# Log-sum-exp kernel: the heads of the last fourteen tiles shared out anew among four engines, three TensorE heads in the last row, no waits between the PSUM banks of a pair

## Chip, cores and metric

One core of a Trainium2 chip. The metric is the device time of one execution in microseconds (us), the median of several; the kernel before takes 327.5 us. The profiled span of the same execution is about 1.8 us shorter than its time.

## The reference, cut to what matters

```python
B, S, D, H = 8, 2048, 2048, 8          # x: (B, S, D) float32, bias: (H, D // H)
x_heads = x.reshape(B, S, H, D // H).transpose(0, 2, 1, 3) + bias[None, :, None, :]
x_tiled = np.repeat(x_heads, 2, axis=2)
mx = x_tiled.max(axis=-1, keepdims=True)
lse = mx.squeeze(-1) + np.log(np.exp(x_tiled - mx).sum(axis=-1))   # (8, 8, 4096)
```

Each of the 8 x 2048 rows holds 8 heads of 256 numbers. For every head: add a bias vector, exponentiate, sum, take the logarithm, write it twice. 134 MB are read, 1 MB is written.

## The kernel before, as far as it matters here

64 tiles of 2 MB (128 partitions x 2 rows x 2048), nine buffers. A head can be done in three ways, and the kernel shares the eight heads of a row among the engines by stage:

- **TensorE head**: TensorE puts the bias into a PSUM bank (a matmul of ones with three bf16 parts of the bias) and adds x (a matmul with the identity, float32). ScalarE exponentiates and sums in one instruction.
- **Weighted head**: ScalarE exponentiates x alone; VectorE multiplies by exp(bias), which lies in PSUM, and sums.
- **Added head**: GpSimd adds the bias in SBUF, ScalarE exponentiates, VectorE reduces.

```python
BULK = dict(pe=3, acc=1, g0=4, late=True, fold=0)        # whole tiles, 3 TensorE heads, 4 added
MIXED = dict(pe=1, acc=1, g0=4, late=False, fold=0)      # 1 TensorE head, 3 weighted, 4 added
PROMPT = dict(pe=2, acc=2, g0=8, late=False, fold=0)     # 2 TensorE heads, 6 weighted
PROMPT_F1 = dict(pe=2, acc=2, g0=8, late=False, fold=1)  # the last head folded by GpSimd
PROMPT_F2 = dict(pe=2, acc=2, g0=8, late=False, fold=2)  # the last two
STAGES = [
    (0, (BULK,)), (50, (MIXED,)),
    (56, (MIXED, MIXED)),                                # from here half tiles, one row each
    (61, (PROMPT, PROMPT)), (62, (PROMPT, PROMPT_F1)), (63, (PROMPT_F2, PROMPT)),
]
LAST_COLS = [                                            # column pieces of the two last rows
    [(0, 512), (1280, 2048), (512, 1280)],
    [(0, 512), (512, 1024), (1024, 1536), (1536, 2048)],
]
...
pairs = [pp.tile([P, 2 * MM], F32, name=f"pair{i}") for i in range(2)]
ps = [p[:, c : c + MM] for p in pairs for c in (0, MM)]  # four banks in two tiles of two banks
...
def sum_biased(m, t, k, p, mm, sums):                    # ScalarE's part of a TensorE head
    for h in range(m["pe"]):
        c = h * Dh
        act = nc.scalar.activation(out=xts[t % NBUF][:, k, c : c + Dh], in_=p[:, c : c + Dh],
            func=ACT.Exp, accum_out=sums[:, k, h : h + 1])
        last_uses[t].append(on_x(t, act, [mm]))
...
def fold(t, k, h0, h1, sums, after):                     # GpSimd: times exp(bias), then 256 -> 32
    v = xts[t % NBUF][:, k, h0 * Dh : h1 * Dh]
    done = nc.gpsimd.tensor_tensor(out=v, in0=v, in1=w_sb[...], op=ALU.mult)
    ...
    while n > FOLD:
        n //= 2
        done = nc.gpsimd.tensor_tensor(out=v[:, :, 0:n], in0=v[:, :, 0:n],
                                       in1=v[:, :, n : 2 * n], op=ALU.add)
    # VectorE sums the remaining 32, one unit later
```

For one half tile the order is: TensorE adds x and puts the next half's bias; ScalarE exponentiates the weighted heads of this half, then does the TensorE heads of the half before; VectorE weighs.

The softmax here doesn't subtract the row's maximum and nothing guards it: scores larger than these inputs give would overflow.

## Time and profile before

| | kernel before |
|---|---|
| time, median (range) | 327.52 us (327.40 to 327.56) |
| busy: TensorE, VectorE, ScalarE, GpSimd | 77%, 88%, 81%, 89% |
| DMA rate over the span | 416 GB/s |
| last piece of x lands | 319.45 us |
| sums complete | 322.00 us |
| span | 325.5 us |

How to read it: four engines look nearly full, yet none of them sets the pace over the 300 us in the middle; the loads do, and nine buffers keep them some 30 us ahead. So I read the end: the last landings, the chain behind them, and the TensorE clock there. The lines stand in the prediction. In them L307 is ScalarE's exponential of x, L282 its part of the TensorE heads, L342 a weighted head on VectorE, L326 and L372 VectorE's reductions, L358 GpSimd's fold, and L408 the closing transpose.

The median of 327.52 us is that of the three executions known when the prediction was written; a fourth, run with the changed kernel, makes it 327.46 (the table after the prediction).

### The profile page before, as it was taken

What the parts mean: (1) busy time and instruction counts of PE and PEld (TensorE: products, weight loads), DVE (VectorE), ACT (ScalarE), POOL (GpSimd) and SP (SyncE); (2) the same over time, 40 slices, a digit from 0 to 9 for tenths busy, and PEclk for the clock granted to TensorE, in tenths of its full rate; (3) what the DMA queues carried; (4) which work ended last, traced back from release to release, by engine and by line L of the source; (5) the groups of instructions that cost most, each with busy time, mean ns of one, the idle gap of its engine ahead of it and who ended that gap; (6) DMA issues with size and microseconds to landing.
All of it is one profiled execution on the core that took longest, in us unless ns stands there. A gap on an engine that the chain in (4) does not pass through costs nothing.

```text
span 325.5 us, 2113 instructions
## 1 busy us (share of the span) xinstructions
PE 250.0 (77%) x541; PEld 86.9 (27%) x541; DVE 285.9 (88%) x320; ACT 264.3 (81%) x421; POOL 289.9 (89%) x88
## 2 busy tenths in 40 slices
PE   4478999499987888777879797889788455576792
PEld 1123333233322323223323232223223101122220
DVE  1006999999999999999898899989998999999995
ACT  1119999499978969888787978697879897799995
POOL 6999999799999999999999999999999999999713
PEclk9999999899979979998997989797979855555558
DMA  8999999999999999999999999999999999999994
GB/s 293 427 431 429 431 429 424 431 427 429 429 429 429 427 426 429 429 423 430 432 425 429 431 422 427 431 427 429 429 431 425 429 432 424 413 422 421 422 400 143
DMA packets 11806, 135.42 MB, mean 416 GB/s; under 512 B 1361, under 2 KB 1489, under 8 KB 2833
## 3 DMA queue, kind: packets, MB, share of 16 engines
q1 hardware_dynamic: 11696, 135.27, 98.6%
q8 instruction: 4, 0.07, 0.1%
q14 instruction: 8, 0.07, 0.0%
q10 hardware_dynamic: 2, 0.01, 0.0%
q0 software_dynamic: 96, 0.00, 0.0%
HBM read 134.23 MB, written 1.05 MB: 416 GB/s over the span
## 4 chain that ended last, share of the span: by engine, by line
DMA 48%; DVE 33%; ACT 8%; POOL 6%; PE 3%; issue 1%; SPq 0%; DVEq 0%
DMA xt<-in_x_dram 45%; DVE R L326 27%; ACT xt L307 6%; DVE xt L319 4%; POOL xt L301 4%; DMA b<-bparts 2%; PE pair L249 1%; PE one_ps L249 1%; DVE xt L342 1%; ACT xt L282 1%; DMA brow<-in_bias_dram 1%; ACT xt L267 1%; POOL brest L173 1%; POOL brest L171 1%; PE pair L203 0%
## 5 line engine op out<-in xcount | busy, mean ns | idle before, releaser
L301 POOL TENSOR_TENSOR xt<-xt,b_rep 128x2048 f32<-128x2048 f32 (+1 forms) x66 | 277.3, 4210 | 18.9 <-DMA xt<-in_x_dram 18.9
L326 DVE TENSOR_REDUCE R<-xt 128x14 f32<-128x3584 f32 (+1 forms) x56 | 208.1, 3716 | 2.6 <-ACT xt L307 0.9
L307 ACT ACTIVATE xt<-xt 128x2560 f32<-128x2560 f32 (+3 forms) x91 | 164.2, 1828 | 14.8 <-POOL xt L301 14.3
L249 PE MATMUL pair<-xt,ident 128*128 128x512 f32 x200 | 105.5, 654 | 0.0
L249 PE MATMUL one_ps<-xt,ident 128*128 128x512 f32 x100 | 61.0, 695 | 19.9 <-DMA xt<-in_x_dram 19.8
L267 ACT ACTIVATE xt<-pair 128x1024 f32<-128x1024 f32 x50 | 52.3, 1045 | 17.2 <-PE pair L249 15.8
L249 PEld LDWEIGHTS pair<-xt,ident 128*128 128x128 f32 x200 | 42.4, 212 | 56.0 <-issue 56.0
L319 DVE TENSOR_TENSOR xt<-xt,w_ps 128x512 f32<-128x512 f32 x50 | 34.0, 680 | 25.6 <-ACT xt L307 25.4
L233 PE MATMUL pair<-xt,ident 128*128 128x512 f32 (+1 forms) x44 | 34.0, 872 | 21.2 <-DMA xt<-in_x_dram 18.2
L260 ACT ACTIVATE xt<-one_ps 128x256 f32<-128x256 f32 x100 | 37.7, 394 | 8.1 <-PE one_ps L249 8.1
L203 PE MATMUL one_ps<-b,ones 3*128 3x512 bf16 x50 | 19.0, 381 | 17.9 <-ACT xt L260 11.8
L203 PEld LDWEIGHTS <-ones 3*128 3x128 bf16 x150 | 12.5, 92 | 65.7 <-issue 59.7
L203 PE MATMUL pair<-b,ones 3*128 3x512 bf16 x100 | 29.9, 378 | 0.0
L249 PEld LDWEIGHTS one_ps<-xt,ident 128*128 128x128 f32 x100 | 15.6, 197 | 41.3 <-DMA xt<-in_x_dram 34.1
L260 ACT ACTIVATION_READ_ACCUMULATOR xt<-one_ps 128x1 f32 x100 | 22.1, 221 | 0.0
L342 DVE CUSTOM_DVE_ANT_0 xt<-xt,one_ps 128x256 f32<-128x256 f32 x50 | 19.1, 414 | 0.3 <-ACT xt L307 0.3
L233 PEld LDWEIGHTS pair<-xt,ident 128*128 128x128 f32 x44 | 10.4, 294 | 29.6 <-DMA xt<-in_x_dram 19.7
L342 DVE CUSTOM_DVE_ANT_0 xt<-xt,w_ps 128x256 f32<-128x256 f32 x45 | 17.5, 417 | 0.0
L282 ACT ACTIVATE xt<-pair 128x256 f32<-128x256 f32 x34 | 12.5, 374 | 0.1
L326 DVE TENSOR_REDUCE R_last<-xt 128x4 f32<-128x1024 f32 x10 | 12.1, 1214 | 0.0
L218 PE MATMUL pair<-b,ones 3*128 3x512 bf16 (+1 forms) x22 | 10.2, 465 | 1.1 <-ACT xt L267 1.1
L358 POOL TENSOR_TENSOR xt<-xt,w_sb 128x256 f32<-128x256 f32 (+1 forms) x2 | 2.1, 1026 | 8.7 <-ACT xt L307 8.5
(38 smaller groups left out, 55.9 us busy)
## 6 DMA issues: line engine op xcount, KB each, us to landing
xt<-in_x_dram SPq DMA_DIRECT2D x56, 2048.0 KB, 29.9
xt<-in_x_dram SPq DMA_DIRECT2D x14, 1024.0 KB, 21.0
xt<-in_x_dram SPq DMA_DIRECT2D x5, 256.0 KB, 11.4
out_dram<-res SPq DMA_DIRECT2D x1, 896.0 KB, 7.3
xt<-in_x_dram SPq DMA_DIRECT2D x2, 384.0 KB, 16.5
out_dram<-res_last SPq DMA_DIRECT2D x1, 128.0 KB, 1.7
b<-bparts POOLq DMA_DIRECT2D x3, 1.5 KB, 6.5
brow<-in_bias_dram ACTq DMA_DIRECT2D x1, 8.0 KB
```

Source lines behind the costliest of these rows:

```text
L203: nc.tensor.matmul(p, lhsT=ones3, rhs=each_row(b3, h * Dh, Dh, K), start=True, stop=False,)
L218: nc.tensor.matmul(p, lhsT=ones3, rhs=each_row(b3, 0, n, kb - ka), start=True, stop=False,)
L233: mm = nc.tensor.matmul(p, lhsT=ident, rhs=xts[t % NBUF][:, ka:kb, 0:n], start=False, stop=True,)
L249: mm = nc.tensor.matmul(p, lhsT=ident, rhs=xts[t % NBUF][:, :, h * Dh : (h + 1) * Dh], start=False, stop=True,)
L260: act = nc.scalar.activation(out=xts[t % NBUF][:, k, 0:Dh], in_=got[0][:, k * Dh : (k + 1) * Dh], func=ACT.Exp, accum_out=sums[:, k, 0:1],)
L267: act = nc.scalar.activation(out=xts[t % NBUF][:, :, Dh : m["pe"] * Dh].rearrange("p k (h j) -> p h k j", j=Dh), in_=got[-1].rearrange("p ...
L282: act = nc.scalar.activation(out=xts[t % NBUF][:, k, c : c + Dh], in_=p[:, c : c + Dh], func=ACT.Exp, accum_out=sums[:, k, h : h + 1],)
L301: add = nc.gpsimd.tensor_tensor(out=v, in0=v, in1=each_row(b_rep, c - G0, D - c, k1 - k0), op=ALU.add)
L307: return on_x(t, nc.scalar.activation(out=v, in_=v, func=ACT.Exp), [after])
L319: mul = nc.vector.tensor_tensor(out=f, in0=f, in1=each_row(w_ps, m["pe"] * Dh - W0, n, k1 - k0), op=ALU.mult,)
L326: red = nc.vector.tensor_reduce(out=sums[:, k0:k1, h0:H], in_=v.rearrange("p k (h j) -> p k h j", j=Dh), op=ALU.add, axis=mybir.AxisListTy ...
L342: ttr = nc.vector.tensor_tensor_reduce(out=v, in0=v, in1=w, scale=1.0, scalar=0.0, op0=ALU.mult, op1=ALU.add, accum_out=dst,)
```

## The change

The intent: keep the cheap bulk stage longer, relieve GpSimd of its slow bias adds in the half tiles, and use all engines evenly in the last tile.

```diff
-PROMPT = dict(pe=2, acc=2, g0=8, late=False, fold=0)
+SINGLE_F1 = dict(pe=1, acc=1, g0=8, late=False, fold=1)
+TRIPLE = dict(pe=3, acc=3, g0=8, late=False, fold=0)
 STAGES = [
     (0, (BULK,)),
-    (50, (MIXED,)),
-    (56, (MIXED, MIXED)),
-    (61, (PROMPT, PROMPT)),
-    (62, (PROMPT, PROMPT_F1)),
-    (63, (PROMPT_F2, PROMPT)),
+    (54, (MIXED,)),
+    (57, (PROMPT_F1, PROMPT_F1)),
+    (62, (SINGLE_F1, SINGLE_F1)),
+    (63, (PROMPT_F2, TRIPLE)),
 ]
 LAST_COLS = [
     [(0, 512), (1280, 2048), (512, 1280)],
-    [(0, 512), (512, 1024), (1024, 1536), (1536, 2048)],
+    [(0, 512), (768, 1280), (1280, 1792), (512, 768), (1792, 2048)],
 ]
...
+    bank_users = [[], []]
+    def on_bank(i, ins):
+        for j, u in bank_users[i // 2]:
+            if j != i and u.ins.engine != ins.ins.engine:
+                tc.declare_no_dep(ins.ins, u.ins, reason="another bank")
+        bank_users[i // 2].append((i, ins))
+        return ins
... (put_bias, add_x and sum_biased call it; a row of three heads takes two banks; the
...  TensorE heads of a row may now come in two pieces)
```

## The prediction

> **What bounds the kernel now.** I read the page first, for engine shares and the slices, then the chain that ended last, then the timelines of single engines over the last 20 us, then the groups by form.
>
> The page (PEclk is the granted TensorE clock in tenths, GB/s the DMA rate, 40 slices of 8.1 us):
>
> ```profile
> span 325.5 us, 2113 instructions
> PEclk9999999899979979998997989797979855555558
> GB/s 293 427 431 429 431 429 424 431 427 429 429 429 429 427 426 429 429 423 430 432 425 429 431 422 427 431 427 429 429 431 425 429 432 424 413 422 421 422 400 143
> HBM read 134.23 MB, written 1.05 MB: 416 GB/s over the span
> ```
>
> From the second slice to the last but one the rate is flat: 134 MB of input pass at some 428 GB/s, and no edit of who computes what changes the bytes. The trace's record of landings says the same: whole tiles (2 MB) land 4.89 us apart, half tiles 2.48 us apart, and the last piece of x lands at 319.45 us. The loads run six or more tiles ahead, so a late engine in the middle costs nothing. What remains to win or lose is what follows the last landings. The second thing to see is the clock: half from slice 32 on, in the stage that this change rebuilds.
>
> The chain that ended last (start, us, what), from 305 us on:
>
> ```profile
> 294.41 19.82 DMA xt<-in_x_dram
> ...
> 314.26 1.48 ACT xt L307
> 315.74 1.46 ACT xt L282 x8
> 317.20 1.47 ACT xt L307 x2
> ...
> 318.69 0.42 DVE xt L342
> ...
> 321.86 0.14 DVE R_last L372
> 322.00 0.14 issue
> 322.14 0.32 PE tpair L408
> ```
>
> DMA sets the time until tile 62's second half lands (314.24). Then ScalarE has a queue, its four TensorE heads lying ahead of the exponentials of the last tile, and VectorE starts the last nine heads only at 318.69. The sums are complete at 322.00; transpose, logarithm, store and end take another 3.5 us (325.5 - 322.0), which the change leaves alone. So I ask one thing: when are the sums complete afterwards?
>
> Timeline of TensorE (L218 writes the bias, L233 adds x; start, busy us):
>
> ```profile
> 299.36 1.22 PE L233 MATMUL pair<-xt,ident 128*128 128x256 f32 x2 [0.93 <-DMA xt<-in_x_dram]
> 300.51 0.39 PE L218 MATMUL pair<-b,ones 3*128 3x256 bf16 x1
> ...
> 309.36 2.08 PE L233 MATMUL pair<-xt,ident 128*128 128x512 f32 x2
> 311.37 0.60 PE L218 MATMUL pair<-b,ones 3*128 3x512 bf16 x1
> 311.90 2.08 PE L233 MATMUL pair<-xt,ident 128*128 128x512 f32 x2
> ...
> 317.89 1.12 PE L233 MATMUL pair<-xt,ident 128*128 128x512 f32 x2
> ```
>
> At half clock two heads hold TensorE for 2.01 us (309.36 to 311.37) and their bias for 0.53 (to 311.90), 2.54 us a half tile against 2.48 of DMA; one head takes 1.15 (299.36 to 300.51). At full clock, from 315.9 on, two heads take 1.12.
>
> Groups by form (busy us, mean ns):
>
> ```profile
> L342 DVE CUSTOM_DVE_ANT_0 xt<-xt,w_ps 128x256 f32<-128x256 f32 x45 | 17.5, 417 | 0.0
> L326 DVE TENSOR_REDUCE R<-xt 128x8 f32<-128x2048 f32 x6 | 13.7, 2283 | 0.9 <-ACT xt L307 0.9
> L307 ACT ACTIVATE xt<-xt 128x1536 f32<-128x1536 f32 x10 | 14.6, 1471 | 0.3 <-DMA xt<-in_x_dram 0.3
> L307 ACT ACTIVATE xt<-xt 128x768 f32<-128x768 f32 x12 | 9.9, 835 | 0.0
> L358 POOL TENSOR_TENSOR xt<-xt,w_sb 128x256 f32<-128x256 f32 x1 | 0.8, 779 | 8.5 <-ACT xt L307 8.5
> ```
>
> These give the unit costs. A weighted head on VectorE is 417 ns, and such heads start 0.343 us apart (318.69 to 321.78 for nine). An exponential of 1536 elements is 1.47 us, of 768 0.835, so 0.83 ns an element; in a row each starts 0.09 us before the last one ends. A TensorE head summed by ScalarE takes 0.36 us in a row, and the last one ends 0.5 us after its start. A one-head fold on GpSimd is 0.78 us and three adds, 2.12 us from start to next possible start.
>
> **What the Trainium skill says.** "TensorE: Matmul & The Clock Gate", Part 1: half clock is the idle state, judged in free-running windows of about 3.4 us. The trace agrees: every change of the granted clock lies on a 3.41 us grid. Summing in each window the matmuls that add x, I find that 0.99 and more of a half-clock window was followed by full clock, 0.84 was not; at full clock 0.56 and less was followed by half, 0.59 was not. "SBUF - State Buffer", Who interferes with whom: a VectorE instruction with two SBUF inputs contends with GpSimd's reads, one with a single SBUF input doesn't. The weights of heads 2 to 6 lie in PSUM, and the trace agrees: the heads keep 0.34 us beside GpSimd's adds (270 to 281 us) and without them. "PSUM - Partial Sum Buffer", bank collisions: guard by bank and quadrant; dropping waits between different banks is allowed. No wait of this kind is large in the trace: TensorE's L233 waited for ScalarE once, 3.0 us.
>
> **The change part by part.**
>
> Stages. Bulk runs to tile 53 instead of 49, the mixed whole tiles are 54 to 56, half tiles begin at 57. Bulk VectorE work is 0.60 + 3.89 = 4.5 us a tile against 4.89 of DMA, so this part stays hidden. One split fewer saves 2 x 2.48 - 4.89 = 0.07 us of DMA.
>
> GpSimd's bias add. Ten half-tile adds of 2.36 us go, and with them on ScalarE a second exponential (1024 elements) and on VectorE a reduce of 1.21 us per half. In their place each half of tiles 57 to 61 costs VectorE 5 x 0.343 + about 0.17 (last reduce of the fold) = 1.9 us (before 3 x 0.343 + 1.21 - about 0.08 = 2.15), ScalarE 1.39 + 2 x 0.36 = 2.1, GpSimd 2.12, all under 2.48. At half clock TensorE is at 2.54 and falls behind by 0.06 a half, 0.6 in ten, which tile 62 with one head makes up.
>
> Do they arrive in time? In the kernel before VectorE starts the first mixed tile 7.2 us after its landing (261.75 - 254.54). Afterwards that start is 274.55 + 7.2 = 281.75. Three mixed tiles at 4.24 end at 294.5, ten halves at 1.9 at 313.5, the six heads and reduce of tile 62's first half at 315.7. GpSimd: its last add ends at 284.4 + 4.54 = 288.9, the first fold starts at about 292.3 (after two exponentials), eleven folds of 2.12 end at 315.6. ScalarE: 62's second half, 1792 elements, lands at 314.2 and is through at 314.2 + 1.69 = 315.9. All three meet within 0.4 us there; no backlog, and no reserve either.
>
> The end, VectorE. From 315.9: six heads and a reduce to 318.2, then heads 5; 2, 3, 4; 3, 4; 5, 6; 7: nine times 0.343 = 3.09, to 321.3, and the last reduce 0.2: 321.5. That is 0.5 us better than 322.00: one head of tile 62 comes to VectorE, ScalarE's queue shrinks by two heads.
>
> The end, ScalarE. Exponential to 315.8, two heads of tile 62 to 316.5, 768 + 768 elements to 318.0, row 0's two heads to 318.7, then 512, 512 and 256 elements (0.52, 0.52, 0.31) to 320.06, three heads of the last row, the last starting at 320.8: 321.3, if TensorE has delivered.
>
> The end, TensorE. With one head in tile 62 TensorE's share of x falls to 1.15 / 2.48 = 0.46, so by the windows above the half clock will stand in the last tile, where the kernel before had full clock, earned by two heads in each of tiles 61 and 62. In order from the landing at 314.2: one head 1.15, bias 0.53, row 0's two heads 2.01, bias of the last row on two banks 0.9, its first two heads 2.01, its third 1.2: 322.0. ScalarE then needs 0.5 for the last head: 322.5. At full clock the same order waits for landings only and TensorE is done by 319.8.
>
> Sum: sums complete at max(321.5, 321.3, 322.5) = 322.5 instead of 322.0 at half clock, and 321.5 at full clock: 327.52 + 0.5 = 328.0 or 327.52 - 0.5 = 327.0.
>
> **The rivals.** (1) Full clock at the end: the ten two-head halves hold TensorE at 100% at half clock, so the clock will go up in some windows of 287 to 312. But at full clock two heads fill 1.12 / 2.48 = 0.45, and it falls again; to have it at 318 the window rule must fail. Partly, a full window up to about 315.9 would save 0.7 us of the TensorE row: 327.5. (2) VectorE or GpSimd is late: with a fold of 2.3 us instead of 2.12 eleven of them end at 317.6, two us late, and the end moves by about as much, to 328.5 to 329. For it: one fold only is measured, and VectorE's last reduce waited 0.2 us for it. Against: nothing in the trace slows GpSimd beside PSUM-weighted heads. (3) The waits between banks were costing more than the single 3.0 us: then the end could be earlier, but before 314 nothing waits for anything but DMA. (4) The last load's smaller pieces (128 KB) land later: the pieces cost 0.64 per 256 KB now against 0.61 at full rate, so 0.1 us at most.
>
> **Range and chances.** I give half clock in the tail about 6 in 10 (328.0), part 2 to 3 (327.5), full the rest (327.0), and add 0.3 us for the chip and for rival 2. Predicted 327.8 us, eight in ten between 326.8 and 328.6. Two per cent is 6.5 us; the whole reach of the change is the 2.6 us between the last landing and the complete sums, plus a backlog that the deep load queue hides. Faster 0.01, within 2% 0.98, slower 0.01.
>
> **What would show it right or wrong.** The rate stays 428 GB/s and the last piece lands near 319.4. In the last 10 us: PEclk (half or full?), L233's third head of the last row ending near 322 and ScalarE's last heads waiting for TensorE, in the chain of waits TensorE instead of VectorE before the transpose. VectorE's first head of tile 62's second half should start at about 315.9; if it starts a microsecond later, the step of the meeting engines failed. If L372 waits for GpSimd in every half, rival 2 holds. If the clock is full to the end and the time is 327.0, the window step failed. A load that waits for a buffer, or a time beyond 330, would upset the whole picture.

## The result, and the profile after

| | before | after |
|---|---|---|
| time, median (range) | 327.46 us (327.27 to 327.56) | 327.40 us (327.31 to 327.84) |
| runs | 4 | 4 |
| ratio after to before, 95% interval | | 1.0001 (0.9984 to 1.0019) |

A ratio here is the mean time of one kernel's runs over that of the other's of the same rounds, so not quite the ratio of the medians quoted beside it. The time lies within the predicted range and within 2%, and no difference from the kernel before is shown. It hides two things, a slower and a faster end, and the profiles show both.

The page of the kernel after, in the execution that was profiled (327.84 us):

```profile
span 326.0 us, 2182 instructions
PEclk9999999779995999799799979978997797657755
HBM read 134.23 MB, written 1.05 MB: 415 GB/s over the span
```

The DMA rate is as before; TensorE ends at half clock. The chain that ended last in this execution (start, us, what):

```profile
294.61 19.87 DMA xt<-in_x_dram
...
314.52 1.22 PE pair L249 x2
315.75 0.53 PE pair L231
316.28 2.01 PE pair L249 x2
318.29 0.75 PE pair L231 x2
319.04 2.02 PE pair L249 x2
...
321.08 0.84 ACT xt L298 x4
...
321.93 0.48 ACT xt L298 x2
```

Here L249 adds x, L231 puts a bias, L298 is ScalarE's part of the TensorE heads; further down L323 is ScalarE's exponential of x, L358 a weighted head on VectorE, L388 VectorE's last reduce, L424 the closing transpose. Before, ScalarE and VectorE filled this stretch; now TensorE leads from the landing of tile 62's second half at 314.48 to 321.06, and the last row's third head is summed at 322.4 us. VectorE's own last reduce was over at 321.7 us. The list of waits (engine, line, what it waited for: us in total, times, longest) has just one such entry:

```profile
ACT xt L298 <- PE pair L249: 0.6, 1, 0.6
```

A second profile of the very same kernel (the first experiment, 326.78 us) has another chain:

```profile
294.40 19.85 DMA xt<-in_x_dram
...
314.28 1.71 ACT xt L323
...
316.01 0.42 DVE xt L358
...
321.34 0.14 DVE R_last L388
...
321.62 0.32 PE tpair L424
```

Here the tail is VectorE's fifteen weighted heads, and the sums are complete at 321.5. The landing came 0.23 us earlier there; the rest of the difference goes with the clock, and e1 and e3 below test whether it is the cause. Time table of the two executions and of the third experiment below, one stretch each (the columns are the stretch, its length, busy time and count of TensorE, its weight loads, VectorE, ScalarE and GpSimd, then granted clock, DMA share and GB/s):

```profile
316.00:320.00 4.00, 4.00 (x7) 1.15 (x7) 3.77 (x22) 4.00 (x13) 3.41 (x6) 0.50 1.03 313
```

```profile
316.00:320.00 4.00, 3.90 (x8) 1.09 (x8) 3.99 (x24) 4.00 (x13) 3.63 (x6) 0.77 1.04 328
```

```profile
316.00:320.00 4.00, 3.02 (x8) 0.70 (x6) 4.00 (x24) 4.00 (x13) 3.67 (x6) 1.00 1.04 330
```

At clock 0.50 TensorE is busy all the time (VectorE and ScalarE nearly so: ScalarE's one wait for TensorE, 0.6 us, comes only at 321.1), at 0.77 VectorE just leads, at 1.00 TensorE has time to spare.

### The profile page after: what moved, and what is told of

Its sections match the earlier page's. It is cut to its first block, busy times and chain, and to the rows that moved or that the text cites. A ratio compares the mean times of both kernels' runs of the same rounds, so it can differ in the third digit from the quotient of the medians.

```text
span 326.0 us, 2182 instructions
## 1 busy us (share of the span) xinstructions
PE 263.2 (81%) x565; PEld 90.5 (28%) x565; DVE 283.8 (87%) x306; ACT 263.6 (81%) x425; POOL 290.5 (89%) x123
## 4 chain that ended last, share of the span: by engine, by line
DVE 41%; DMA 39%; PE 7%; ACT 6%; POOL 5%; issue 1%; SPq 0%
DVE R L342 36%; DMA xt<-in_x_dram 36%; DVE xt L335 6%; ACT xt L323 4%; PE pair L267 3%; POOL xt L317 3%; DMA b<-bparts 2%; PE one_ps L267 2%; PE pair L249 2%; ACT xt L285 1%; DMA brow<-in_bias_dram 1%; ACT xt L298 1%; POOL brest L173 1%; POOL brest L171 1%; PE pair L231 0%
## 5 line engine op out<-in xcount | busy, mean ns | idle before, releaser
L317 POOL TENSOR_TENSOR xt<-xt,b_rep 128x2048 f32<-128x2048 f32 x57 | 258.7, 4542 | 19.6 <-DMA xt<-in_x_dram 19.6
L342 DVE TENSOR_REDUCE R<-xt 128x14 f32<-128x3584 f32 (+1 forms) x56 | 214.5, 3830 | 1.9
L323 ACT ACTIVATE xt<-xt 128x2560 f32<-128x2560 f32 (+5 forms) x77 | 158.5, 2068 | 10.9 <-POOL xt L317 10.6
L267 PE MATMUL pair<-xt,ident 128*128 128x512 f32 x216 | 116.3, 666 | 0.0
L267 PE MATMUL one_ps<-xt,ident 128*128 128x512 f32 x108 | 65.8, 694 | 21.2 <-DMA xt<-in_x_dram 21.2
L285 ACT ACTIVATE xt<-pair 128x1024 f32<-128x1024 f32 x54 | 56.7, 1050 | 19.9 <-PE pair L267 18.5
L249 PE MATMUL pair<-xt,ident 128*128 128x512 f32 (+1 forms) x36 | 30.3, 946 | 7.8 <-DMA xt<-in_x_dram 7.6
L358 DVE CUSTOM_DVE_ANT_0 xt<-xt,w_ps 128x256 f32<-128x256 f32 x61 | 22.4, 418 | 0.0
L382 POOL TENSOR_TENSOR xt<-xt 128x128 f32<-128x128 f32 (+3 forms) x39 | 13.9, 356 | 3.1
L374 POOL TENSOR_TENSOR xt<-xt,w_sb 128x256 f32<-128x256 f32 (+1 forms) x13 | 10.0, 773 | 5.2 <-ACT xt L323 4.5
L298 ACT ACTIVATE xt<-pair 128x256 f32<-128x256 f32 x33 | 12.4, 389 | 0.6 <-PE pair L249 0.6
L249 PEld LDWEIGHTS pair<-xt,ident 128*128 128x128 f32 x36 | 8.2, 278 | 16.7 <-DMA xt<-in_x_dram 13.1
L358 DVE CUSTOM_DVE_ANT_0 xt<-xt,one_ps 128x256 f32<-128x256 f32 x27 | 10.6, 415 | 0.5 <-ACT xt L323 0.5
```

Source lines behind the costliest of these rows:

```text
L249: mm = nc.tensor.matmul(p, lhsT=ident, rhs=xts[t % NBUF][:, ka:kb, c : c + w], start=False, stop=True,)
L267: mm = nc.tensor.matmul(p, lhsT=ident, rhs=xts[t % NBUF][:, :, h * Dh : (h + 1) * Dh], start=False, stop=True,)
L285: act = nc.scalar.activation(out=xts[t % NBUF][:, :, Dh : m["pe"] * Dh].rearrange("p k (h j) -> p h k j", j=Dh), in_=got[-1].rearrange("p ...
L298: act = nc.scalar.activation(out=xts[t % NBUF][:, k, h * Dh : (h + 1) * Dh], in_=p, func=ACT.Exp, accum_out=sums[:, k, h : h + 1],)
L317: add = nc.gpsimd.tensor_tensor(out=v, in0=v, in1=each_row(b_rep, c - G0, D - c, k1 - k0), op=ALU.add)
L323: return on_x(t, nc.scalar.activation(out=v, in_=v, func=ACT.Exp), [after])
```

## The experiments

Theory A: the loads set the time until tile 62's second half lands; from there the end is the later of VectorE's row of heads (about 7.3 us) and TensorE's row, which at half clock is longer. Rival B: TensorE has no part in the end, VectorE or the last landing sets it. Rival C: the waits between banks never bind. Rival D: full clock alone would be worth as much in the kernel before.

Twelve runs in three groups, each group on one chip beside the kernel before, five rounds each. "Length" is from the landing of tile 62's second half to TensorE's closing transpose, read from the profiled execution; it takes out the scatter of the landing itself, which in the fourteen profiles falls between 314.06 and 314.61 us. Each length is one execution, but profiles with the same chain agree to 0.01 us: 7.98 in after and e6, 7.37, 7.37 and 7.36 in c_after, e3 and e8, 7.71 and 7.70 in e2 and e10.

| run | median (range), us | ratio to before (95%) | clock in the tail | length, us |
|---|---|---|---|---|
| before, first profile | 327.52 (327.40 to 327.56) | | full from 315.9 | 7.90 |
| after, first profile | 327.40 (327.31 to 327.84) | 1.0001 (0.9984 to 1.0019) | half | 7.98 |
| c_after | 327.41 (326.78 to 327.71) | 0.9994 (0.9981 to 1.0006) | full from 317.8 | 7.37 |
| e1_light_pe | 326.94 (326.84 to 327.25) | 0.9985 (0.9972 to 0.9999) | half | 7.37 |
| e2_two_last | 327.45 (327.28 to 327.55) | 0.9998 (0.9985 to 1.0010) | half to 319.9 | 7.71 |
| e3_hot_pe | 326.79 (326.67 to 326.93) | 0.9978 (0.9966 to 0.9991) | full | 7.37 |
| e4_waits | 328.53 (328.36 to 328.82) | 1.0032 (1.0019 to 1.0045) | half | 9.14 |
| e5_mixed_halves | 328.88 (328.36 to 329.07) | 1.0035 (1.0021 to 1.0048) | half | 9.38 |
| e6_bulk_50 | 327.45 (327.37 to 327.71) | 0.9999 (0.9986 to 1.0011) | half | 7.98 |
| e7_two_62 | 327.31 (326.99 to 328.29) | 0.9998 (0.9985 to 1.0011) | half | 8.83 |
| e8_hot_again | 326.78 (326.54 to 327.04) | 0.9979 (0.9967 to 0.9992) | full to 321.5 | 7.36 |
| e9_before_hot | 327.57 (327.14 to 327.67) | 1.0001 (0.9988 to 1.0013) | full | 8.10 |
| e10_hot_two_last | 327.37 (327.27 to 327.89) | 0.9996 (0.9982 to 1.0010) | full to 321.1 | 7.70 |
| e11_hot_waits | 327.30 (326.99 to 327.39) | 0.9993 (0.9980 to 1.0005) | full to 321.7 | 7.88 |

The kernel before had medians of 327.49, 327.48 and 327.49 us in the three groups, so medians of different groups are set beside each other below.

**c_after: the changed kernel again, nothing edited**

> The changed kernel again, as the yardstick of this chip. If the tail's TensorE clock decides (theory A), the timed runs scatter with their mean granted clock, 0.877 with about 327.8 us and 0.895 with about 327.3, and the median is 327.3 to 327.6, a ratio of 0.999 to 1.001 to the kernel before. If the clock has no part in it (rival B: the end is set by VectorE at 321.7 us in every run), the times don't go with the clock.

The two executions with profiles lie at the ends of the scatter: 327.84 us with half clock to the end and length 7.98, 326.78 with full clock from 317.8 and length 7.37. The first four runs went with their mean clock (327.84 us at 0.877, 327.45 at 0.884, 327.31 and 327.35 at 0.895), but these were known when the expectation was written. The five new ones hardly do: 327.41 at 0.884, 327.71 at 0.890, and 326.78, 327.15 and 327.48 all at 0.900. So this part of the expectation was not met. The mean over 326 us says little of the clock in the last 10, and the landing scatters too; what decides between theory A and rival B are e1 and e3. The kernel has at least two ends, and its median says little about either.

**e1_light_pe: TensorE's work in the last tile made lighter, inexact on purpose**

```diff
+    ident_h = sb.tile([P, P], BF16, name="ident_h")        # copied from ident by VectorE
+            rhs = xts[t % NBUF][:, ka:kb, c : c + w]
+            if t == T - 1:
+                rhs = rhs.bitcast(BF16).rearrange("p k (w two) -> p k w two", two=2)[:, :, :, 1]
             mm = nc.tensor.matmul(
-                lhsT=ident, rhs=xts[t % NBUF][:, ka:kb, c : c + w],
+                lhsT=ident_h if t == T - 1 else ident, rhs=rhs,
```

> The last tile's TensorE matmuls read only the upper half of each x[...], inexact on purpose; every other instruction stays. Theory A (TensorE at half clock sets the end: 1.22 + 0.53 + 2.01 + 0.75 + 2.02 + 0.84 us from the landing of tile 62's second half): TensorE is done about 319.5 instead of 321.9, ScalarE's last head no longer waits and the sums end with VectorE at 321.7 instead of 322.4, 0.7 us less than the profiled run of after, the median about 327.0. Rival B (VectorE or the last landing sets the end anyway): no change, 327.3 to 327.6.

Adding x for two heads took 0.54 us in this tail instead of 2.01. The chain, and the same stretch of the time table as above:

```profile
294.24 19.83 DMA xt<-in_x_dram
...
321.15 0.14 DVE R_last L393
...
321.43 0.46 PE tpair L429
```

```profile
316.00:320.00 4.00, 2.10 (x5) 0.33 (x4) 4.00 (x24) 4.00 (x14) 3.61 (x7) 0.50 1.03 329
```

The clock was half in the whole tail, and yet the length is that of the full-clock execution, 7.37, with VectorE at the end; the median is 0.47 us below c_after's. The sums are within the reference's tolerance, but only the upper half of each float is read: this is a probe, no version to keep. It shows that at half clock it is TensorE's work, and no other engine, that makes the end late. Rival B falls.

**e2_two_last: two TensorE heads in the last row instead of three**

```diff
-    (63, (PROMPT_F2, TRIPLE)),
+    (63, (PROMPT_F2, dict(TRIPLE, pe=2, acc=2))),
```

> The last row has two TensorE heads again, so undoing the third head. Theory A at half clock: TensorE done at 321.0, ScalarE at 321.9, VectorE has one head more and ends at 322.05: sums at 322.05, 0.35 us earlier than in the profiled run of after and the same in every clock state, median about 327.4. If TensorE were no bound (rival B) the extra VectorE head makes it 0.34 us slower, about 327.7.

As theory A has it: VectorE ends the chain, 7.71 long, between the two states of the three-head kernel (7.37 and 7.98), and the runs lie within 0.27 us of each other against 0.93 for c_after. By the lengths the third head costs 0.27 us at half clock (7.98 against 7.71) and gains 0.34 at full clock (7.37 against 7.71, and e10 below); the medians show no difference (327.45 and 327.41).

**e3_hot_pe: useless matmuls to hold the clock up**

```diff
                     bias_there = put_bias(*next_units.pop(0))
+                    if 59 <= t < T - 1:
+                        for _ in range(2 if (t, k0) == (62, 0) else 1):
+                            nc.tensor.matmul(tpair[:, 0].rearrange("p k q -> p (k q)"),
+                                lhsT=ident, rhs=w_sb[:, 0:Dh], start=True, stop=True)
```

> Eight useless matmuls (256 columns, constant data) are put behind the bias from tile 59 to tile 62, to keep the TensorE share above 0.6 of a window. Theory A: the clock goes to full near 300 us and stays full to about 318; TensorE is done before 320.5, sums end with VectorE at 321.7, median about 327.0, and the scatter between runs shrinks. If the clock doesn't rise, TensorE falls behind by over a microsecond per half tile and the time is 329 to 334. Rival B: no gain at full clock, 327.4.

The clock is full from 288.7 to 322.9 us: it rose before the first useless matmul (298.1 us), and with them it stayed up. By the edit and the trace there are nine, not the eight of the expectation. The length is 7.37, the scatter 0.26 us, the median 0.70 us below the kernel before; the interval of the ratio lies clear of 1. TensorE in this execution (start, us; L486 is the useless work):

```profile
315.21 0.70 PE L486 MATMUL tpair<-w_sb,ident 128*128 128x256 f32 x2
315.75 1.02 PE L249 MATMUL pair<-xt,ident 128*128 128x512 f32 x2
316.70 0.49 PE L231 MATMUL pair<-b,ones 3*128 3x512 bf16 x2
317.56 1.12 PE L249 MATMUL pair<-xt,ident 128*128 128x512 f32 x2 [0.36 <-DMA xt<-in_x_dram]
319.17 0.70 PE L249 MATMUL pair<-xt,ident 128*128 128x256 f32 x2 [0.48 <-DMA xt<-in_x_dram]
```

It does more work and still waits for DMA twice, where in the first profile it was 2.2 us late with the third head (321.9 against a landing at 319.4 plus 0.3 of work).

**e4_waits: the waits between banks of a pair put back**

```diff
         for j, u in bank_users[i // 2]:
-            if j != i and u.ins.engine != ins.ins.engine:
-                tc.declare_no_dep(ins.ins, u.ins, reason="another bank")
+            pass
```

> The changed kernel with the waits between banks of a pair back. Theory A: ScalarE's head of tile 62's second half then waits for the matmuls of the next unit (the same pair, the other bank), which at half clock end 3.8 us after that half's landing, where it now reads 2.0 us after it; the ScalarE queue behind it slips by 1.5 to 1.8 us and the sums end some 1.0 us later at half clock, not at all at full clock: median 327.7 to 328.3. Rival C (the waits never bind, since before 314 us everything waits for DMA alone): 327.4, as after.

1.1 us slower than c_after's median, and 0.2 beyond the expected range. ScalarE's timeline, in brackets the idle time before and what ended it:

```profile
315.91 0.37 ACT L298 ACTIVATE xt<-pair 128x256 f32<-128x256 f32 x1
...
318.12 0.38 ACT L298 ACTIVATE xt<-pair 128x256 f32<-128x256 f32 x1 [1.76 <-PE pair L249]
318.50 0.83 ACT L323 ACTIVATE xt<-xt 128x768 f32<-128x768 f32 x1
```

The head at 318.12 was ready at 315.6, when its own matmul was over. It waited for the matmuls of the next row, which write the other bank of the pair, and everything queued behind it slipped. The length grows by 1.16 us against the half-clock execution of after. Rival C falls for the new order of work. That the waits cost nothing in the kernel before is not tested; its chain shows none. What they cost at full clock e11 was meant to size.

**e5_mixed_halves: tiles 57 to 61 with the old half tiles**

```diff
-    (57, (PROMPT_F1, PROMPT_F1)),
+    (57, (MIXED, MIXED)),
```

> Tiles 57 to 61 keep the old half tiles (GpSimd adds the bias of four heads, VectorE three weighted heads and a reduce, 2.15 us a half on VectorE against 1.80 measured for the new ones). If the fold stage is what lets the longer bulk be caught up, VectorE arrives at tile 62 at 294.96 + 10 x 2.15 = 316.5 instead of 313.7 and starts the second half's heads at 318.6 instead of 316.2: sums 2.0 to 2.4 us later, median 329.0 to 329.6. If the load queue hides it (rival: only the last landing counts): 327.4.

1.5 us slower than c_after, somewhat less than expected, because VectorE came to tile 62 at 315.90 instead of the 316.5 that I had worked out. (The chain below counts that start from the end of the instruction before, 315.98.) It shows VectorE alone in the whole window asked, from before 312 us to the closing transpose:

```profile
312.70 1.14 DVE R_last L342
313.83 0.33 DVE xt L358
...
314.85 1.13 DVE R_last L342
315.98 0.33 DVE xt L358
```

The second half's heads start at 318.04, where they start at 316.23 in after. So the fold stage is what lets the longer bulk be caught up in time; by itself it brings no time, it prevents a loss.

**e6_bulk_50: the mixed whole tiles from tile 50 again**

```diff
-    (54, (MIXED,)),
+    (50, (MIXED,)),
```

> The mixed whole tiles begin at 50 again, all else as after. Theory A: the tail hangs on the landing of tile 62's second half, so nothing changes: median 327.2 to 327.6, scatter as after. Should the longer bulk be what costs or gains, it would move by 0.3 or more.

No difference, and in its profile the chain of after: TensorE at half clock, length 7.98. Four more bulk tiles neither cost nor gain.

**e7_two_62: no stage with a single TensorE head**

```diff
-    (62, (SINGLE_F1, SINGLE_F1)),
```

> Tile 62 keeps two TensorE heads (no stage with one). VectorE has five heads in place of six there and would end at 320.9 after a landing at 314.25; ScalarE has 0.5 us more to do and would end at 321.9 at full clock; at half clock the TensorE row is 0.86 us longer and begins up to 0.6 late: sums 323.0 to 323.5. Theory A: median 327.5 to 328.3, slower than after in the half state. If the single-head stage only cost the clock, TensorE would be at full clock more often and the median 327.2 or less.

The widest scatter of all, 326.99 to 328.29. The profiled execution is the slowest (328.29): half clock, length 8.83, TensorE from the landing to ScalarE's last heads, sums complete at 322.9 (expected for the half state: 323.0 to 323.5). The median of 327.31 is better than I expected, nearer the other reading, so on the mean this run is inconclusive; that the single-head stage takes 0.85 us off the half-clock case (8.83 to 7.98) is shown by the two profiles alone.

**e8_hot_again: e3 repeated on another group**

> The changed kernel with eight useless matmuls again, as the yardstick of this chip and to see whether its gain repeats: 326.6 to 327.0 us in every run, ratio 0.997 to 0.999, clock full from before 316 to past 319 us.

It repeats: 326.78, ratio 0.9979, all ten runs of e3 and e8 between 326.54 and 327.04.

**e9_before_hot: useless matmuls in the kernel before**

```diff
                     bias_there = put_bias(*next_units.pop(0))
+                    if 58 <= t < T - 1:
+                        for _ in range(2 if m["pe"] == 1 else 1):
+                            nc.tensor.matmul(tpair[:, 0]..., lhsT=ident, rhs=w_sb[:, 0:Dh], ...)
```

> The kernel before with useless matmuls of 256 columns from tile 58 to 62 (two per half tile where one head is TensorE's, one where two are). Theory A: in the kernel before the end is set by ScalarE's queue and VectorE's last nine heads, not by TensorE, so full clock gains nothing: 327.3 to 327.6. The changed kernel at full clock is then 0.5 to 0.7 us faster than this one. If full clock alone were the gain (rival D), this one too would come to 326.8.

327.57 against 327.49: full clock gains nothing there, and rival D falls. (The kernel before had full clock from 315.9 us in its own profile; what e9 adds is full clock in the half tiles, from 298.4 us.) The length of 8.10 is 0.2 over that of before; the chain of waits shows VectorE busy without a break from 300 us to the end in this execution. That the useless work itself set ScalarE and thus VectorE back at the start would fit, but isn't shown. At full clock the changed kernel (e8) is 0.79 us faster by the medians.

**e10_hot_two_last: e3 and e2 together**

> Two TensorE heads in the last row, at full clock. Theory A: VectorE has one head more and sets the end: 0.34 us later than with three heads at full clock, 327.0 to 327.2. So the third head is worth 0.3 us once the clock is full, where it cost about as much at half clock.

The length is 0.34 us over that of e8 (7.70 to 7.36), as expected, the median 0.59 us higher and above the expected 327.0 to 327.2; 0.25 us of that I can't attribute (the landing of this profiled execution is 0.29 us later than e8's, and the intervals of the two ratios overlap).

**e11_hot_waits: e3 and e4 together**

> The waits between banks of a pair back, at full clock. The head of tile 62's second half then waits for row 0's matmuls, which end at 316.8 where it read at 316.2: 0.6 us on ScalarE's queue, which ends at 321.9 instead of 321.3 against VectorE's 321.45: 0.3 to 0.5 us slower than the same kernel without the waits, 327.1 to 327.3, against 1.1 us measured at half clock.

0.52 us in both the median and the length (7.88 to 7.36). But the probe itself stands in the path that it measures. Lines of TensorE and of ScalarE:

```profile
315.14 0.70 PE L486 MATMUL tpair<-w_sb,ident 128*128 128x256 f32 x2
315.67 1.02 PE L249 MATMUL pair<-xt,ident 128*128 128x512 f32 x2
316.73 0.38 ACT L298 ACTIVATE xt<-pair 128x256 f32<-128x256 f32 x1 [0.50 <-PE pair L249]
```

ScalarE waits 0.50 us for row 0's matmuls, and these were held up by 0.63 us of useless work put before them (the row's data had landed at 314.79). Without it they would have ended some 0.6 us earlier, before ScalarE came to this head: an estimate from this trace. So the half microsecond is what the waits cost the kernel with the probe; without useless matmuls they may well cost nothing at full clock, as e4's expectation had it. No run has full clock without them and the waits back, so that stays open. The 1.16 us at half clock, from two profiles without useless work, stands.

## Why the prediction was right

That the number came out says little: the range was 1.8 us wide, the kernel before lies in it too, and within 2% is 6.5 us. The prediction leaned to 0.3 us slower; measured is no difference. What can be judged are its steps.

**The bound.** Right: 415 GB/s, the chain runs through DMA up to tile 62's second half, the last piece of x lands at 319.7 and 319.5 in the two profiles (predicted 319.4).

**The unit costs.** Right. The fold that the kernel before had shown once stands twelve times (busy us, mean ns):

```profile
L358 DVE CUSTOM_DVE_ANT_0 xt<-xt,w_ps 128x256 f32<-128x256 f32 x61 | 22.4, 418 | 0.0
L374 POOL TENSOR_TENSOR xt<-xt,w_sb 128x256 f32<-128x256 f32 x12 | 8.8, 731 | 5.2 <-ACT xt L323 4.5
L388 DVE TENSOR_REDUCE R_last<-xt 128x1 f32<-128x32 f32 x12 | 2.2, 184 | 0.2 <-POOL xt L382 0.2
```

A fold every 2.09 us (2.12 predicted), 1.80 us of VectorE a half tile (1.9 predicted), and VectorE waited 0.2 us for GpSimd in all: rival 2 of the prediction is out. A weighted head costs 418 ns here, and 411 to 418 each in the kernel before, beside GpSimd's adds and while GpSimd stood idle (307.3 to 315.8), which agrees with the Trainium skill, "SBUF — State Buffer", Who interferes with whom.

**The meeting of three engines at 315.9.** Right: VectorE's first head of tile 62's second half starts at 316.23 and 316.01, 1.75 us after its landing both times (1.7 predicted), with 0.26 us of waiting for ScalarE before it in the first profile. There was no backlog, and e5 shows that with the old half tiles there would have been.

**VectorE's end.** Right: 7.2 us from the landing to the last reduce in both profiles (7.3 predicted).

**TensorE at half clock.** The step was right in kind: the chain went through TensorE and ScalarE's last head, as named. Its size was 8.3 us from landing to complete sums, against 7.9 measured. Two terms of the sum were too large: the last row's bias on two banks took 0.75 us instead of 0.9, and for the third head with ScalarE's part I had put 1.2 + 0.5 behind one another, where the chain has 0.85 + 0.48.

**The clock's chance.** Here a step was too strict. I wrote that the half clock "will stand in the last tile", and that for a full clock "the window rule must fail". The rule did not fail. In the second profile the window from 314.4 to 317.8 us, at half clock, was filled by the last tile's own matmuls, a share of 0.99, and full clock followed; in the first the window lay at 314.2 to 317.7, its share was 0.90, and it didn't. I had looked only at what the single-head stage does to a window, not at the last tile's. That the place of the windows relative to the landing decides the end is argued from these two profiles and not shown: in e6 a window began with the landing (314.06), its share was 0.97, and the clock stayed half. The limits that I had read from one trace are softer in all fourteen (see the last section). The weights of the prediction (half 6 in 10) make 327.7 of its three times, not 327.8, and I can't find in it the 0.3 us that the text says it adds; it came out 0.4 us above the measured median. Two profiles of this kernel, one in each state, can't test the weights.

**The waits.** The prediction held that before 314 nothing waits for anything but DMA and gave the removed waits no gain. The kernel before has one such wait of TensorE for ScalarE, 3.0 us before 259.85, of which 0.4 lie behind the landing that it needed too (259.44), and none on its chain; no run tested it without the waits. What the prediction left out, as e4 shows, is that the new order needs them gone.

So the expected half microsecond did not vanish in one place. The new sharing takes it off VectorE and ScalarE, and in the executions in which TensorE's clock is half at the end TensorE gives it back. With the clock held up more than that is there: 326.8 against 327.5, the fastest of all versions tried, and both halves of the statement were tested from the other side (e1: half clock, light work; e9: full clock, old sharing).

## What to carry to other kernels

When work is moved onto TensorE near the end of a kernel, cost it at both clocks, and look at the clock that the stages before it leave. (That the single-head stage takes the clock from the last tile was the prediction's reasoning; no run shows it, and e7, without that stage, had half clock in its tail too.) A median that doesn't move can be a mixture of two ends; the length from the last decisive landing to the end, and the granted clock beside it, separate them where the time cannot. Waits that show no cost in one order of work can cost a microsecond in another, so size them in the order in which they will stand, and see that the probe does not lengthen what is waited for.

## What the Trainium skill lacked or had wrong

- "TensorE: Matmul & The Clock Gate", Part 1, names an idle and a busy window of about 3.4 us without saying how busy. I summed the recorded durations of all matmuls but the bias ones in each window of the fourteen profiles (records of neighbours overlap, so a share can exceed 1, and reaches 1.4). At half clock none of 117 windows with a share under 0.96 was followed by full clock, and all 134 of 1.04 and more were; of the 28 between, 20 were. At full clock all 141 windows under 0.52 were followed by half clock, and none above 0.65 was; between these the outcome is mixed, 23 of the 157 windows from 0.52 to 0.65 being followed by half clock, the highest at 0.643, and others from 0.535 on staying full. So a window that is half full can already lose the clock; it need not be idle. (The page's part on psum-queue depth-cycling tells of a clock that oscillates with micro-idles, but gives no share.)
- The same table gives full clock after one busy window (about 3.4 us sustained). In the last 45 us of the fourteen profiles there are 20 half-clock windows in which TensorE was busy for at least 97% by its records, but only 0.79 to 0.95 without the bias; none was followed by full clock. So the bias matmuls, with three rows of weights, seem not to count: an inference from these windows, which no run tested.
- "PSUM — Partial Sum Buffer", bank collisions, advises to guard by bank. No page says what a wait that guards by a tile of two banks costs: 1.16 us at half clock in this tail (e4 against after), and at full clock 0.5 us with the useless matmuls in its path (e11).
- "DMA: Bandwidth & Descriptors" has nothing on the scatter of a steady stream: the same half tile landed between 314.06 and 314.61 us in fourteen profiles, as much as the change is worth.
